# S5 parameter tables in compact form, passed from engine to engine one job slot later

## The chip, the core and the metric

The kernel runs on one core of one Trainium2 chip. A core has TensorE (PE in the profile, its weight loads PEld), VectorE (DVE), ScalarE (ACT), GpSimd (POOL) and SyncE (SP), which here issues every DMA. Each engine works through its own queue in order and waits for the others by semaphores. The metric is the device time of one execution in microseconds (us), as a median over runs.

## What is computed

One step of a two-layer decoder for 512 prompt tokens and 8 x 4 sample tokens, 544 columns in all, model width 1024. Layer 0 mixes tokens by gated linear attention, layer 1 by an S5 state-space layer; each is followed by a squared-ReLU MLP of width 4096. All of it is normed before and after, in fp32:

```
x = x + post_norm(mixer(pre_norm(x)))
x = x + post_norm(square(relu(pre_norm(x) @ w_up)) @ w_down)
```

The change concerns the parameters of the S5 mixer. Of 64 groups with 64 complex states and 16 channels each:

```
dt = exp(log_step);  mag = exp(ar * dt)
lam = mag * (cos(ai * dt) + i sin(ai * dt))
z = (lam - 1) / (ar + i ai);  bb = z * b
h[t] = lam * h[t-1] + bb @ u[t];  y[t] = Re(c @ h[t]) + d * u[t]
```

The kernel does four time steps at once. For that it needs, per pair of groups, W (z times powers of lam times b, to bring four steps of u into the state), Q (powers of lam times c, to read the state out), K (c lam^k bb between the four steps, with d on its diagonal) and the cosine and sine of the angle of lam^4 at 128 multiples, by which states are turned so that the recurrence itself is real.

## The kernel before

**Jobs.** Weights come as 184 tiles of 128 x 1024 fp32. Each tile is split into two parts that TensorE takes: `wh`, the rounded value (a cast by ScalarE, line 111), and `wl = raw - wh` (VectorE line 113, POOL line 115). The activations are split likewise, into a high and a low part (`xh` and `xl`, in the MLP `hh` and `hl`). A job is one tile times one half of the columns (288 or 256): eight blocks of three products, 24 matmuls on line 186. `PLAN` lists the 368 jobs, in blocks of four tiles (8 jobs) or eight (16 jobs). They are numbered from 0 here; the MLP of layer 0 holds jobs 64 to 191, up and down phases of 16 jobs in turn.

**The split of weights.** `plan()` places each tile's split ahead of its first job, in two halves of 512 columns: a tile has its ring slot (`RING` = 5) only when the tile five places earlier has had its last job. In a steady run of blocks of four, the eight jobs of a block get 1, 1, 1, 0, 0, 1, 2 and 2 halves, and a tile's first job follows its first half by 4 to 7 jobs. `job()` calls `split_w` at a job's start: cast, low part, and with the second half the load of the tile three further on (line 93). `dve_ks` says how many of a half's four 128-column slices VectorE subtracts; POOL does the others.

**A job's end.** `finish()` issues the evacuation of the job's sums, then what was deferred to this job, then one entry of `bg`, the background list. In an up phase the evacuation is r = max(sums, 0) * scale by VectorE (line 350), a square and the cast to `hh` by ScalarE (352, 353), and `hl` = r - hh by VectorE (354, deferred to the end of the same job). In a down phase it is one addition into `acc` by VectorE (362).

**The tables.** `s5_prepare` fills `bg` from job 80: one entry a job. Entries 0 to 10 compute dt, mag, lam, z and masks, mostly on POOL, and end in `z_rows`; seven rests; `z_turn` transposes z on TensorE and sets `dve_ks` to `DD[1]` (before it, it is `DD[0]`). From entry 21 on (job 101) come 16 units of four slots, to job 164; a unit is two pairs of groups:

- slot A: W's products (POOL 1008 and 1009, VectorE 1010 and 1011), the angle's first lines (VectorE 1069 to 1071);
- slot B: W's sums (1016, 1017) and its DMA to the scratch tensor `wd`; the angle's reduction (1077, 1078, 1080, 872); loads for the next unit;
- slot C: Q's products on POOL (1029, 1030); sine on ScalarE (1085), the cosine's argument on VectorE (876 to 878);
- slot D: the K products of the unit before on TensorE (1052), its copy by ScalarE (1055) and diagonal by VectorE (1058); Q on VectorE (1035 to 1038), masked bb by ScalarE (1044), cosine (1089), and their DMAs to `qd`, `md` and `wd`.

The two groups of a pair keep to their own halves of a table by zeros. Before, these zeros go through the arithmetic: masks `gm` are multiplied into z and the powers of lam, and W and Q are computed at full width, zeros with them.

The S5 stage, after the MLP, loads W, Q, K and the angles back, u by u.

Of the kernel before, what the change touches and what calls it, by code (L numbers as in the profile page):

```python
# [55 lines left out]
DD = (4,0)  # L56
# [16 lines left out]
class Builder:  # L73
    def __init__(self, tc, io):
        self.tc, self.nc, self.io = tc, tc.nc, io
        self.jobs = 0
        self.after = defaultdict(list)
        self.before_evac = defaultdict(list)
        self.hold, self.held = set(), []
        self.n_tiles = io["w"].shape[0]  # L80
        self.raw, self.wh, self.wl = {}, {}, {}
        self.tile0 = 0
        self.plan()
        self.dve_ks = 1
        self.bg = []
        self.dve_win = None
        self.part = {}
# [8 lines left out]
    def split_w(self, t, part=None):  # L96
# [7 lines left out]
        if part == 0:  # L104
# [6 lines left out]
        nc.scalar.activation(h[:, a:c], r[:, a:c], AF.Copy)  # L111
# [96 lines left out]
    def finish(self, ps, evac):  # L208
        j = self.jobs
        if j in self.hold:  # L210
# [130 lines left out]
    def mlp(self, g_post, g_next, sink=None, after_first=None, before_last=None):  # L341
# [4 lines left out]
        def up(m, hf, ps):  # L346
# [7 lines left out]
            self.defer(0, lambda: nc.vector.tensor_sub(hl[:, m, c0:c1], r[:, :n], f32(h)))  # L354
# [451 lines left out]
    def s5_prepare(self, ctx):  # L806
# [4 lines left out]
        sm = p.tile([128, 26, 32], F32, name="sm")  # L811
# [4 lines left out]
        ldb = p.tile([128, 2, 32, 16], F32, tag="q", name="ldb")  # L816
        ldc = p.tile([128, 2, 32, 16], F32, name="ldc")
        tmp = p.tile([128, 640], F32, name="tmp")
        gm = p.tile([128, 2], F32, name="gm")
        dsk = p.tile([32, 32], F32, name="dsk")  # L820
        iota = p.tile([128, 128], F32, name="iota")
        lp = p.tile([128, 2, 32, 5], F32, tag="cs", name="lp")
        l5 = p.tile([128, 2, 32, 10], F32, name="l5")
        eye = self.cst[0:32, C_ID:C_ID + 32]

        self.kk = [p.tile([32, 2, 256], F32, name=f"kk{i}") for i in (0,)]

# [115 lines left out]

        def masks():
            for r in (0, 1):
                o = l5[:, r].rearrange("p q (t g) -> p q t g", g=2)
                for g in (0, 1):
                    G.tensor_scalar(o[:, :, :, g], lp[:, r], gm[:, g:g + 1], None, op0=OP.mult)
# [4 lines left out]
        def z_rows():  # L953

            z4 = p.tile([128, 2, 32, 4], F32, tag="w", name="z4")
            zm = p.tile([128, 2, 16, 8, 2], F32, tag="q", name="zm")
# [4 lines left out]
            for r in (0, 1):  # L961
                src = z4[:, r].rearrange("p (u q) s -> p u s q", q=2)
                dst = zm[:, r].rearrange("p u (s g) q -> p u s g q", g=2)
                for g in (0, 1):
                    for q in (0, 1):
                        G.tensor_scalar(dst[:, :, :, g, q], src[:, :, :, q], gm[:, g:g + 1], None, op0=OP.mult)
            st["zm"] = zm

        def z_turn():
# [3 lines left out]
            zt = p.tile([128, 512], F32, tag="zb", name="zt")  # L973
            for i in range(4):
                r, hf = divmod(i, 2)
                nc.tensor.transpose(ps[:, i * 128:(i + 1) * 128],
                                    zm[:, r, 8 * hf:8 * hf + 8].rearrange("p u s q -> p (u s q)"),
                                    self.cst[:, C_ID:C_ID + 128])
            nc.scalar.activation(zt, ps, AF.Copy)
            for i in range(4):  # L980
                r, hf = divmod(i, 2)
                nc.sync.dma_start(zd[8 * hf:8 * hf + 8, :, r].rearrange("u s q n -> (u s) q n"),
                                  zt[:, i * 128:(i + 1) * 128])

        def bbar():
            o = p.tile([128, 2, 32, 16], F32, name="bb")
            self.bb = o
# [4 lines left out]
            G.tensor_scalar(ldc[:, 1], ldc[:, 1], -1.0, None, op0=OP.mult)  # L992

        def unit_w(u):
            zb = p.tile([128, 2, 2, 128], F32, tag="zb", name="zb")
            bt = p.tile([128, 2, 2, 64], F32, tag="bt", name="bt")
            src = zd[u].rearrange("s r q n -> s (r q n)")[:, None, :].to_broadcast([8, 16, 512])
            nc.sync.dma_start(zb.rearrange("p r q n -> p (r q n)"), src)
            nc.sync.dma_start(bt, io["s5bt"][:, u])
            st["zb"], st["bt"] = zb, bt  # L1000

        def unit_w2(u):
            w = p.tile([128, 2, 2, 2, 64], F32, tag="w", name="w")
            zb = st["zb"].rearrange("p r q (g n) -> p r q g n", g=2)
            b = [st["bt"][:, r, :, None, :].to_broadcast([128, 2, 2, 64]) for r in (0, 1)]
            zr, zi = zb[:, 0], zb[:, 1]
            tp = [tmp[:, 256 * i:256 * (i + 1)].rearrange("p (q g n) -> p q g n", q=2, g=2) for i in (0, 1)]
            G.tensor_mul(tp[0], zi, b[1])
            G.tensor_mul(tp[1], zi, b[0])
            V.tensor_mul(w[:, 0], zr, b[0])  # L1010
            V.tensor_mul(w[:, 1], zr, b[1])
            st["w"], st["tp"] = w, tp

        def unit_w3(u):
            w, tp = st["w"], st["tp"]
            V.tensor_sub(w[:, 0], w[:, 0], tp[0])
# [3 lines left out]
        def q_parts(u):  # L1020
            sh = [128, 2, 10, 16]
            l = [l5[:, r, 2 * u:2 * u + 2, :, None].to_broadcast(sh) for r in (0, 1)]
            c = [ldc[:, r, 2 * u:2 * u + 2, None, :].to_broadcast(sh) for r in (0, 1)]
            tp = [tmp[:, 320 * i:320 * (i + 1)].rearrange("p (q t c) -> p q t c", q=2, t=10) for i in (0, 1)]
            return l, c, tp

        def unit_q0(u):
            l, c, tp = q_parts(u)
            G.tensor_mul(tp[0], l[1], c[1])
            G.tensor_mul(tp[1], l[1], c[0])  # L1030

        def unit_q(u):
            q5 = p.tile([128, 2, 2, 10, 16], F32, tag="q", name="q5")
            l, c, tp = q_parts(u)
# [4 lines left out]
            nc.sync.dma_start(self.qd[u].rearrange("p (a b) -> p a b", a=4),  # L1039
                              q5.rearrange("p r q t c -> p (r q) (t c)")[:, :, 0:128])  # L1040
            bbd = p.tile([128, 2, 2, 2, 16], F32, tag="bbd", name="bbd")
            for r in (0, 1):
                for g in (0, 1):
                    nc.scalar.activation(bbd[:, r, :, g], self.bb[:, r, 2 * u:2 * u + 2], AF.Copy, scale=gm[:, g:g + 1])
            st["q5"], st["bbd"] = q5, bbd

        def unit_k(u):
            ps = self.bank("kp")
            q5, bbd = st["q5"], st["bbd"]
            for q in (0, 1):  # L1050
                for r in (0, 1):
                    nc.tensor.matmul(ps[0:32, q * 128:(q + 1) * 128], bbd[:, r, q].rearrange("p g c -> p (g c)"),
                                     q5[:, r, q, 2:10].rearrange("p t c -> p (t c)"), start=(r == 0), stop=(r == 1))
            kk = self.kk[0]
            nc.scalar.activation(kk[:, :, 0:128], ps[0:32, 0:256].rearrange("p (q n) -> p q n", q=2), AF.Copy)
            for q in (0, 1):
                o = kk[:, q, 96:128]
                V.scalar_tensor_tensor(o, eye, dsk[:, 2 * u + q:2 * u + q + 1], o, op0=OP.mult, op1=OP.add)
                nc.sync.dma_start(self.md[2 * u + q], kk[:, q])

        E1 = np.float32(np.round(2 * np.pi * 16384) / 16384)
        E2 = float(2 * np.pi - float(E1))

        def unit_t(u):
# [3 lines left out]
            for q in (0, 1):  # L1068
                V.tensor_scalar(m[:, q], iota, col("ptu", q), MAGIC, op0=OP.mult, op1=OP.add)
                V.tensor_scalar(a[:, q], iota, col("phi", q), None, op0=OP.mult)  # L1070
            V.tensor_scalar(m, m, MAGIC, None, op0=OP.subtract)
            st["a"], st["m"] = a, m

        def unit_t2(u):
            a, m = st["a"], st["m"]
            col = lambda n, q: t(n)[:, 2 * u + q:2 * u + q + 1]
            V.scalar_tensor_tensor(a, m, -float(E1), a, op0=OP.mult, op1=OP.add)
            V.scalar_tensor_tensor(a, m, -E2, a, op0=OP.mult, op1=OP.add)
            for q in (0, 1):
                V.scalar_tensor_tensor(a[:, q], iota, col("plo", q), a[:, q], op0=OP.mult, op1=OP.add)  # L1080
            sin_arg(V, a)

        def unit_s(u):
            st["cs"] = p.tile([128, 2, 2, 128], F32, tag="cs", name="cs")
            nc.scalar.activation(st["cs"][:, 1], st["a"], AF.Sin)
            cos_arg(V, st["a"], st["m"])

        def unit_c(u):
# [433 lines left out]
```

## Time and profile before

| what | value |
|---|---|
| median of 3 runs | 1404.31 us (1402.98 to 1405.43) |
| the profiled execution | 1405.15 us; its span, first to last instruction, 1403.4 us |
| granted TensorE clock, mean | 0.968 |
| DMA | 157.53 MB in 79274 packets, 112 GB/s |

The page's groups read: line, engine, operation, written tile <- read tiles, shapes, count | busy us of the group, mean ns of one | idle us of the engine just before, and what ended it. A row of the waits reads: who waited <- for whom: us in total, times, longest. A row of the timeline reads: start us, us, engine, line, operation, and in brackets how long the engine sat idle before it and what ended that. A busy TensorE is not one at its peak: matmuls overlap, so a matmul of 290 ns starts 119 to 133 ns after the one before. It slows down when the granted clock falls.

### The profile page before, as it was taken

The numbers are of one execution on the slowest core, as the hardware profiler recorded it, in microseconds if no ns is written. First come the engines' busy times: TensorE is split into PE (matmuls) and PEld (weight loads), VectorE is DVE, ScalarE is ACT, GpSimd is POOL, SyncE is SP. The second block draws the span as 40 slices with busy tenths as digits, with TensorE's granted clock in tenths as the row PEclk, the third lists the DMA queues.
The fourth block names the chain that finished last, engine by engine and source line by source line (L and its number), as shares of the span: only waits on it lengthen the run. The fifth ranks groups of instructions, "written<-read, shape, count | busy, mean of one in ns | idle before, by whom it ended". The sixth has DMA issues, their size and how long they took to land. (4 is left out here: it accounts for less than half of the span.)

```text
span 1403.4 us, 25744 instructions
## 1 busy us (share of the span) xinstructions
PE 1312.2 (94%) x9968; PEld 1278.3 (91%) x9968; DVE 874.9 (62%) x1793; ACT 563.5 (40%) x1283; POOL 639.5 (46%) x715
## 2 busy tenths in 40 slices
PE   7999999989999898889898997899899999999996
PEld 6999999979999797789897997899799999999996
DVE  7865655597437997799648789655871342332345
ACT  6534354645333423323443332344452432432432
POOL 4443344565474674466445343443643333333240
PEclk9999999999999899999999999999999999999998
DMA  5233222312333454445332768432223232323221
GB/s 184 95 120 124 76 95 64 121 61 77 109 109 113 134 162 132 130 141 175 117 106 72 239 183 254 132 99 91 85 66 91 73 109 69 98 76 106 76 61 64
DMA packets 79274, 157.53 MB, mean 112 GB/s; under 512 B 8144, under 2 KB 41808, under 8 KB 78128
## 3 DMA queue, kind: packets, MB, share of 16 engines
q1 hardware_dynamic: 79152, 155.89, 35.6%
q8 instruction: 78, 1.28, 0.4%
q14 instruction: 44, 0.36, 0.1%
HBM read 130.27 MB, written 25.59 MB: 111 GB/s over the span
## 5 line engine op out<-in xcount | busy, mean ns | idle before, releaser
L115 POOL TENSOR_TENSOR wl<-raw,wh 128x384 fp32r<-128x384 f32 (+2 forms) x351 | 422.4, 1217 | 483.9 <-ACT wh L111 482.1
L111 ACT ACTIVATE wh<-raw 128x512 fp32r<-128x512 f32 x368 | 216.3, 618 | 86.5 <-PE held L186 53.4
L186 PE MATMUL held<-xh,wh 128*128 128x288 f32 (+1 forms) x784 | 233.0, 297 | 2.9 <-ACT wh L111 2.8
L186 PE MATMUL held<-xh,wl 128*128 128x288 f32 (+1 forms) x784 | 229.7, 293 | 3.8 <-POOL wl L115 3.8
L186 PE MATMUL held<-xl,wh 128*128 128x288 f32 (+1 forms) x784 | 230.1, 294 | 0.8 <-DVE xl L279 0.8
L186 PE MATMUL mm<-xh,wh 128*128 128x256 f32 (+1 forms) x752 | 221.8, 295 | 0.8 <-ACT wh L111 0.8
L186 PE MATMUL mm<-xl,wh 128*128 128x256 f32 (+1 forms) x752 | 220.1, 293 | 2.1 <-DVE xl L279 2.0
L186 PE MATMUL mm<-xh,wl 128*128 128x256 f32 (+1 forms) x752 | 218.5, 290 | 0.9 <-POOL wl L115 0.9
L113 DVE TENSOR_TENSOR wl<-raw,wh 128x128 fp32r<-128x128 f32 (+2 forms) x247 | 138.2, 568 | 105.6 <-ACT wh L111 100.2
L186 PEld LDWEIGHTS held<-xh,wl 128*128 128x128 f32 x784 | 150.3, 192 | 5.1 <-POOL wl L115 5.1
L186 PEld LDWEIGHTS held<-xh,wh 128*128 128x128 f32 x784 | 150.8, 192 | 4.6 <-ACT wh L111 3.0
L186 PE MATMUL held<-hh,wh 128*128 128x288 f32 (+1 forms) x512 | 150.4, 294 | 4.0 <-ACT wh L111 4.0
L186 PE MATMUL held<-hh,wl 128*128 128x288 f32 (+1 forms) x512 | 150.2, 293 | 3.1 <-POOL wl L115 3.1
L186 PEld LDWEIGHTS held<-xl,wh 128*128 128x128 f32 x784 | 150.7, 192 | 1.4 <-DVE xl L279 1.0
L352 ACT ACTIVATE r<-r 128x256 f32<-128x256 f32 (+1 forms) x128 | 55.1, 431 | 238.3 <-DVE r L350 238.3
L186 PE MATMUL mm<-hh,wh 128*128 128x256 f32 (+1 forms) x512 | 148.8, 291 | 1.7 <-ACT wh L111 1.7
L186 PE MATMUL held<-hl,wh 128*128 128x288 f32 (+1 forms) x512 | 150.0, 293 | 0.0
L186 PE MATMUL mm<-hh,wl 128*128 128x256 f32 (+1 forms) x512 | 148.2, 290 | 1.8 <-POOL wl L115 1.8
L186 PE MATMUL mm<-hl,wh 128*128 128x256 f32 (+1 forms) x512 | 148.8, 291 | 0.0
L186 PEld LDWEIGHTS mm<-xl,wh 128*128 128x128 f32 x752 | 144.8, 193 | 3.4 <-DVE xl L279 3.2
L186 PEld LDWEIGHTS mm<-xh,wh 128*128 128x128 f32 x752 | 145.1, 193 | 2.7 <-issue 1.2
L186 PEld LDWEIGHTS mm<-xh,wl 128*128 128x128 f32 x752 | 144.1, 192 | 1.1 <-POOL wl L115 1.1
(400 smaller groups left out, 2876.1 us busy)
## 6 DMA issues: line engine op xcount, KB each, us to landing
raw<-in_w SPq DMA_DIRECT2D x184, 512.0 KB
S<-in_h SPq DMA_DIRECT2D x4, 1024.0 KB
out_gla_s<-S SPq DMA_DIRECT2D x4, 1024.0 KB
zb<-zd SPq DMA_DIRECT2D x16, 256.0 KB
wd<-w SPq DMA_DIRECT2D x16, 256.0 KB
qd<-q SPq DMA_DIRECT2D x16, 256.0 KB
wd<-cs SPq DMA_DIRECT2D x16, 256.0 KB
qt<-qd SPq DMA_DIRECT2D x16, 256.0 KB
```

Source lines behind the costliest of these rows:

```text
L111: nc.scalar.activation(h[:, a:c], r[:, a:c], AF.Copy)
L113: nc.vector.tensor_sub(l[:, a:b], r[:, a:b], f32(h[:, a:b]))
L115: nc.gpsimd.tensor_sub(l[:, b:c], r[:, b:c], f32(h[:, b:c]))
L186: self.nc.tensor.matmul(ps[:, :c1 - c0], a[:, k], b[:, k, c0:c1], start=(k == 0 and i == 0), stop=(k == KD - 1 and i == 2))
L352: nc.scalar.activation(r[:, :n], r[:, :n], AF.Square)
```

## The change

1. **Compact tables.** W and Q are computed without the zeros (256 and 320 columns a part become 128 and 160). Two ScalarE copies each (`set_blocks`) put the two groups' halves into one buffer, `blk`, that was zeroed once and is written out from there. The masks and the ten-column powers `l5` are gone; `bb` is held twice over, and K is masked once when it leaves PSUM.
2. **Engines and slots.** W's and Q's products all go to VectorE; the angle's first two lines go to ScalarE (with scale and `MAGIC` as bias), its reduction is done in turns (three VectorE steps and a clip), and the cosine is the sine of pi/2 minus the absolute value, all on ScalarE. What one engine makes in one slot, the next uses in a later one. K's zero half in `md` is filled once by a DMA, in slot 10.
3. **Low parts.** `DD` goes from (4,0) to (4,3): in the units VectorE takes three of four slices of every low part, POOL one, where POOL had all four.
4. **Casts.** While `bg` is not empty, `finish` issues the weight casts of the next job before the evacuation. The subtractions stay at the job's start.
5. **hl.** It goes to a list, `late`, that is run after the `bg` entry.
6. The partition order of W's rows changes, and with it the access patterns of `md` and `ud` in the S5 stage.

```diff
-DD = (4,0)
+DD = (4,3)
...
-        nc.scalar.activation(h[:, a:c], r[:, a:c], AF.Copy)
+        if (t, part) not in self.is_cast:
+            nc.scalar.activation(h[:, a:c], r[:, a:c], AF.Copy)
+        if cast_only:
+            self.is_cast.add((t, part))
+            return
...
     def finish(self, ps, evac):
         j = self.jobs
+        if self.bg:
+            for u in self.split_at.get(self.wjob, []):
+                self.split_w(*u, cast_only=True)
...
         if self.bg:
             for f in self.bg.pop(0):
                 f()
+        for f in self.late:
+            f()
+        self.late.clear()
...
-            self.defer(0, lambda: nc.vector.tensor_sub(hl[:, m, c0:c1], r[:, :n], f32(h)))
+            self.late.append(lambda: nc.vector.tensor_sub(hl[:, m, c0:c1], r[:, :n], f32(h)))
...
+        def zeros():
+            G.memset(blk, 0.0)
+            z = blk[0:32, 0:128]
+            nc.sync.dma_start(self.md.rearrange("u r c -> r u c")[:, :, 128:256], z[:, None].to_broadcast([32, 32, 128]))
...
             for r in (0, 1):
-                src = z4[:, r].rearrange("p (u q) s -> p u s q", q=2)
-                dst = zm[:, r].rearrange("p u (s g) q -> p u s g q", g=2)
-                for g in (0, 1):
-                    for q in (0, 1):
-                        G.tensor_scalar(dst[:, :, :, g, q], src[:, :, :, q], gm[:, g:g + 1], None, op0=OP.mult)
+                G.tensor_copy(zm[:, r], z4[:, r].rearrange("p (u q) s -> p u s q", q=2))
...
+        def set_blocks(full, compact):
+            for g in (0, 1):
+                h = slice(64 * g, 64 * g + 64)
+                nc.scalar.activation(full[h, ..., g, :], compact[h], AF.Copy)
...
-            G.tensor_mul(tp[0], zi, b[1])
-            G.tensor_mul(tp[1], zi, b[0])
-            V.tensor_mul(w[:, 0], zr, b[0])
-            V.tensor_mul(w[:, 1], zr, b[1])
+            V.tensor_mul(w, zb[:, 0][:, None].to_broadcast([128, 2, 2, 64]), b)
+            V.tensor_mul(tp, zb[:, 1][:, None].to_broadcast([128, 2, 2, 64]), b)
+            V.tensor_sub(w[:, 0], w[:, 0], tp[:, 1])
+            V.tensor_add(w[:, 1], w[:, 1], tp[:, 0])
...
         def unit_w3(u):
-            V.tensor_sub(w[:, 0], w[:, 0], tp[0])
-            V.tensor_add(w[:, 1], w[:, 1], tp[1])
-            nc.sync.dma_start(self.wd[u][:, 0:512], w.rearrange("p r q g n -> p (r q g n)"))
+            set_blocks(wf, st["w"].rearrange("p r q n -> p (r q) n"))
+            nc.sync.dma_start(self.wd[u][:, 0:512], wf.rearrange("p a g n -> p (a g n)"))
...
+        def unit_k2(u):
+            V.tensor_mul(kk.rearrange("p q (t n) -> p (q t) n", n=32), st["kp"][0:32, 0:256].rearrange("p (a n) -> p a n", n=32),
+                         same.rearrange("p g c -> p (g c)")[:, None].to_broadcast([32, 8, 32]))
...
         def unit_t(u):
             for q in (0, 1):
-                V.tensor_scalar(m[:, q], iota, col("ptu", q), MAGIC, op0=OP.mult, op1=OP.add)
-                V.tensor_scalar(a[:, q], iota, col("phi", q), None, op0=OP.mult)
-            V.tensor_scalar(m, m, MAGIC, None, op0=OP.subtract)
+                nc.scalar.activation(m[:, q], iota, AF.Copy, scale=col("tu", q), bias=MAGIC)
+                nc.scalar.activation(a[:, q], iota, AF.Copy, scale=col("x", q))
...
         def unit_t2(u):
-            V.scalar_tensor_tensor(a, m, -float(E1), a, op0=OP.mult, op1=OP.add)
-            V.scalar_tensor_tensor(a, m, -E2, a, op0=OP.mult, op1=OP.add)
+            V.scalar_tensor_tensor(a, m, MAGIC, a, op0=OP.subtract, op1=OP.subtract)
             for q in (0, 1):
-                V.scalar_tensor_tensor(a[:, q], iota, col("plo", q), a[:, q], op0=OP.mult, op1=OP.add)
-            sin_arg(V, a)
+                V.scalar_tensor_tensor(a[:, q], iota, t("nr")[:, 2 * u + q:2 * u + q + 1], a[:, q], op0=OP.mult, op1=OP.add)
+            V.tensor_scalar(a, a, 0.5, -0.5, op0=OP.min, op1=OP.max)
 
         def unit_s(u):
-            nc.scalar.activation(st["cs"][:, 1], st["a"], AF.Sin)
-            cos_arg(V, st["a"], st["m"])
+            nc.scalar.activation(cs[:, 1], st["a"], AF.Sin, scale=-TURN)
+            nc.scalar.activation(st["m"], st["a"], AF.Abs)
+            nc.scalar.activation(cs[:, 0], st["m"], AF.Sin, scale=-TURN, bias=t("half_pi")[:, 0:1])
...
-        todo = [load, rest, step_size, magnitude, angles, lams, zs, turn_angle, masks, bbar, z_rows,
+        todo = [load, rest, step_size, magnitude, angles, lams, zs, turn_angle, rest, bbar, [z_rows, zeros],
...
-                     [lambda u=u: unit_q0(u), lambda u=u: unit_s(u)],
-                     ([lambda u=u: unit_k(u - 1)] if u else []) + [lambda u=u: unit_q(u), lambda u=u: unit_c(u)]]
-        todo += [rest, rest, lambda: unit_k(15)]
+                     [lambda u=u: unit_q(u), lambda u=u: unit_s(u)] + ([lambda u=u: unit_k(u - 1)] if u else []),
+                     ([lambda u=u: unit_k2(u - 1)] if u else []) + [lambda u=u: unit_q2(u)]]
+        todo += [rest, rest, lambda: unit_k(15), lambda: unit_k2(15)]
```

More of the change, by code (lines that the diff above doesn't have):

```diff
@@ L81, in __init__ @@
         self.raw, self.wh, self.wl = {}, {}, {}
+        self.is_cast, self.late = set(), []
         self.tile0 = 0
@@ L94, in load_raw, with split_w @@
             self.raw[t] = r
-    def split_w(self, t, part=None):
+    def split_w(self, t, part=None, cast_only=False):
         if part is None:
@@ L103, in split_w @@
         r = self.raw[t]
-        if part == 0:
+        if part == 0 and (t, 0) not in self.is_cast:
             pool = self.p_x if self.in_x[t] else self.p_w
@@ L810, in s5_prepare @@
         V, G = nc.vector, nc.gpsimd
-        sm = p.tile([128, 26, 32], F32, name="sm")
+        sm = p.tile([128, 27, 32], F32, name="sm")
         names = {}
@@ L955, in z_rows @@
             z4 = p.tile([128, 2, 32, 4], F32, tag="w", name="z4")
-            zm = p.tile([128, 2, 16, 8, 2], F32, tag="q", name="zm")
+            zm = p.tile([128, 2, 16, 4, 2], F32, tag="q", name="zm")
             sh = [128, 32, 4]
@@ L1000, in unit_w @@
+            nc.sync.dma_start(bt, io["s5bt"][:, u].rearrange("(s e) r q n -> e s (r q n)", s=4))
             st["zb"], st["bt"] = zb, bt
         def unit_w2(u):
[L1003 to L1007, printed above, removed]
@@ L1027, in unit_q0 @@
[L1027 to L1034, printed above, removed]
+            w = p.tile([128, 2, 2, 64], F32, tag="w", name="w")
+            zb, b = st["zb"], st["bt"]
+            tp = tmp[:, :256].rearrange("p (r q n) -> p r q n", r=2, q=2)
+            V.tensor_mul(w, zb[:, 0][:, None].to_broadcast([128, 2, 2, 64]), b)
@@ L1038, in unit_q, with unit_q2 @@
             V.tensor_sub(q5[:, 1], q5[:, 1], tp[1])
[L1039 to L1045, printed above, removed]
+            st["q5"] = q5
+        def unit_q2(u):
+            set_blocks(qf, st["q5"].rearrange("p r q t c -> p (r q) t c"))
+            nc.sync.dma_start(self.qd[u].rearrange("p (a b) -> p a b", a=4), qf.rearrange("p a t g c -> p a (t g c)")[:, :, 0:128])
         def unit_k(u):
-            ps = self.bank("kp")
-            q5, bbd = st["q5"], st["bbd"]
+            ps = st["kp"] = self.bank("kp")
             for q in (0, 1):
                 for r in (0, 1):
[L1052 to L1055, printed above, removed]
+                    nc.tensor.matmul(ps[0:32, q * 128:(q + 1) * 128], self.bb[:, r, 2 * u + q].rearrange("p g c -> p (g c)"),
+                                     qf[:, 2 * r + q, 1:5].rearrange("p t g c -> p (t g c)"), start=(r == 0), stop=(r == 1))
+        def unit_k2(u):
+            V.tensor_mul(kk.rearrange("p q (t n) -> p (q t) n", n=32), st["kp"][0:32, 0:256].rearrange("p (a n) -> p a n", n=32),
+                         same.rearrange("p g c -> p (g c)")[:, None].to_broadcast([32, 8, 32]))
             for q in (0, 1):
@@ L1377, in run @@
             dp = pool("scratch", space=DRAM)
-            self.zd = dp.tile([16, 8, 2, 2, 128], F32, name="zd")
+            self.zd = dp.tile([2, 16, 4, 2, 2, 64], F32, name="zd")
             self.wd = dp.tile([16, 128, 1024], F32, name="wd")
```

103 lines of the change are left out of this document (51 added, 52 removed).

## The prediction

> **What bounds the kernel now.** I read the page first. TensorE is busy nearly all the time, so a change to the S5 tables can only win time where TensorE waits for the engines that make them.
>
> ```profile
> span 1403.4 us, 25744 instructions
> PE 1312.2 (94%) x9968; PEld 1278.3 (91%) x9968; DVE 874.9 (62%) x1793; ACT 563.5 (40%) x1283; POOL 639.5 (46%) x715
> ```
>
> The windows view comes next. I cut it at the first matmul of the layer-0 MLP's first down blocks (353.15), 16 jobs later (401.57) and 80 jobs after that (709.61). The tables are made in these 96 jobs. The columns are length, then busy time and instructions of each engine, the granted clock, and DMA.
>
> ```profile
> core 0: us, PE busy (x) PEld busy (x) DVE busy (x) ACT busy (x) POOL busy (x), PEclk, DMA share, GB/s
> 353.15:401.57 48.42, 48.42 (x387) 48.42 (x386) 20.62 (x58) 17.14 (x38) 30.32 (x75) 1.00 0.32 101
> 401.57:709.61 308.04, 278.62 (x2055) 266.72 (x2054) 246.27 (x498) 111.55 (x288) 174.36 (x156) 0.95 0.43 134
> ```
>
> The first 16 jobs run without a gap, at full clock: 48.42 us, or 3.03 us a job. The next 80 have the same mix, half of 288 and half of 256 columns, so they would need 5 x 48.42 = 242.1 us. In them lie also the small products for K (line 1052):
>
> ```profile
> L1052 PE MATMUL held<-q,bbd 128*32 128x128 f32 x72 | 10.4, 291 | 5.1 <-DVE q L1037 5.1
> L1052 PE MATMUL kp<-q,bbd 128*32 128x128 f32 x56 | 8.5, 295 | 5.4 <-DVE q L1037 5.4
> ```
>
> That is 18.9 us, 1.2 us for each of 16 units. The floor is 242.1 + 18.9 = 261.0 us, against 308.0: 47 us are lost. TensorE is idle for 308.04 - 278.62 = 29.4 us of them; the rest is matmuls at the lower clock that follows each stop (0.95 on average). 47 us is all that this change can win here.
>
> Who causes the loss? First the list of waits over the 80 jobs, then one stop in order of time.
>
> ```profile
> ACT r L352 <- DVE r L350: 112.9, 45, 5.2
> POOL wl L115 <- ACT wh L111: 105.3, 35, 8.7
> DVE hl L354 <- ACT hh L353: 45.3, 47, 1.0
> PE held L186 <- POOL wl L115: 6.9, 8, 1.1
> PE held L186 <- ACT wh L111: 6.8, 3, 2.8
> ```
> ```profile
> 561.26 1.51 DVE L1077 SCALAR_TENSOR_TENSOR ta<-tm,ta 128x256 f32<-128x256 f32 x1
> 562.80 0.84 DVE L1078 SCALAR_TENSOR_TENSOR ta<-tm,ta 128x256 f32<-128x256 f32 x1
> 563.68 0.96 DVE L1080 SCALAR_TENSOR_TENSOR ta<-iota,sm,ta 128x128 f32<-128x128 f32 x2
> 564.89 0.42 DVE L350 SCALAR_TENSOR_TENSOR r<-mm,rs 128x256 f32<-128x256 f32 x1
> 565.34 0.42 ACT L352 ACTIVATE r<-r 128x256 f32<-128x256 f32 x1 [5.16 <-DVE r L350]
> 566.41 0.61 ACT L111 ACTIVATE wh<-raw 128x512 fp32r<-128x512 f32 x1
> 567.08 0.45 PE L186 MATMUL held<-xh,wh 128*128 128x288 f32 x1 [2.79 <-ACT wh L111]
> ```
>
> Read this backwards. TensorE stops at 564.3 for a weight cast (line 111). The cast stands in ScalarE's queue behind the square of an evacuation, which waited 5.16 us for VectorE's r. That r stands in VectorE's queue behind the S5 angles. So VectorE is the bound, and ScalarE, idle itself, carries its delay into the weights. How full VectorE is shows in two units of an up phase, from one K evacuation (549.49) to the next but one:
>
> ```profile
> 549.49:587.34 37.85, 29.66 (x202) 27.63 (x203) 29.69 (x64) 14.50 (x39) 18.10 (x16) 0.91 0.38 122
> ```
>
> A unit takes 37.85 / 2 = 18.9 us. VectorE is busy for 29.69 / 2 = 14.8 of it and waits for hh, as the waits say, 45.3 / 47 = 0.96 us in each of four jobs: 14.8 + 3.9 = 18.7, which leaves nothing. TensorE's work in a unit is four jobs and one K: 4 x 3.03 + 1.2 = 13.3. So an up phase loses 5.6 us a unit. Units fill jobs 101 to 164 in the kernel's numbering, and half of these jobs are up jobs: 8 x 5.6 = 45, nearly the 47 above. In a down job the evacuation is one addition with no wait, and there the engine just keeps up.
>
> **The change part by part.** VectorE first. For a unit of an up phase I count what it does afterwards, with these rows:
>
> ```profile
> L1011 DVE TENSOR_TENSOR w<-zb,bt 128x256 f32<-128x256 f32 x16 | 19.6, 1225 | 0.0
> L1016 DVE TENSOR_TENSOR w<-w,tmp 128x256 f32<-128x256 f32 x16 | 6.6, 414 | 0.0
> L1035 DVE TENSOR_TENSOR q<-l,ldc 128x320 f32<-128x320 f32 x16 | 7.6, 474 | 0.0
> L1080 DVE SCALAR_TENSOR_TENSOR ta<-iota,sm,ta 128x128 f32<-128x128 f32 x32 | 15.4, 521 | 0.6
> L872 DVE TENSOR_SCALAR ta<-ta 128x256 f32<-128x256 f32 x16 | 4.7, 294 | 0.5
> L1058 DVE SCALAR_TENSOR_TENSOR kk<-cst,dsk,kk 32x32 f32<-32x32 f32 x32 | 9.8, 341 | 0.0
> L113 DVE TENSOR_TENSOR wl<-raw,wh 128x512 fp32r<-128x512 f32 x17 | 13.4, 814 | 14.1 <-ACT wh L111 13.9
> L350 DVE SCALAR_TENSOR_TENSOR r<-held,rs 128x288 f32<-128x288 f32 x36 | 16.3, 452 | 19.2 <-PE held L186 19.2
> L354 DVE TENSOR_TENSOR hl<-r,hh 128x288 fp32r<-128x288 f32 x64 | 33.5, 524 | 51.3 <-ACT hh L353 51.3
> ```
>
> From 414 ns at 256 columns and 474 at 320 come estimates for other widths: 0.29 us at 128, 0.32 at 160, 0.53 at 384. Then:
> - w: two products of 256 and two sums of 128, 2 x 0.41 + 2 x 0.29 = 1.4 (W's products with zi come over from POOL; all are half as wide as before).
> - angles: one of 256, two of 128 at 0.52, one clip, 0.41 + 1.04 + 0.29 = 1.75. The four iota lines, three steps of the reduction and the cosine's three steps are gone.
> - q: six of 160, 1.9 (two of them were POOL's).
> - K: the masking product and two diagonals, 0.41 + 0.68 = 1.1.
> - low parts of weights, new here: four of 384 columns, since DD = (4,3) gives VectorE three of every four slices. I take 0.55 each, 2.2; three quarters of the 814 ns row bounds it at 0.61, nothing below 0.53.
> - evacuation: 4 x (0.45 + 0.52) = 3.9.
>
> The sum is 12.2 us. Rows overlap at their ends: for the unit before, the same rows add to 16.6 and the busy time was 14.8, a factor of 0.89. So 10.9 us of VectorE stand against TensorE's 13.3. The wait for hh goes too: hl now stands behind at least one us of slot work, while ScalarE squares and copies. What is late next is then nothing on VectorE, unless POOL gets in its way.
>
> That is the open cost. L1011 is the same instruction as L1016, and takes 1225 ns where POOL runs beside it. Afterwards POOL has only a quarter of each low part:
>
> ```profile
> L654 POOL COPY qkx<-glo 128x128 f32<-128x128 f32 x8 | 3.3, 409 | 0.1
> ```
>
> Four such pieces a unit, each holding VectorE for at most its own 0.41 us, add 1.6: 12.5 us, still under 13.3. The Trainium skill ("SBUF — State Buffer", section "SBUF: two separate sides") says that a VectorE instruction with two SBUF inputs and a POOL instruction exclude each other for the whole instruction; the two rows of w agree. It speaks against this change, which gives VectorE more two-input weight work: by it the whole 1.6 us would stay, and the unit take 12.5 us where the rows alone leave it between 10.9 and 12.5.
>
> ScalarE takes the work over.
>
> ```profile
> L111 ACT ACTIVATE wh<-raw 128x512 fp32r<-128x512 f32 x368 | 216.3, 618 | 86.5 <-PE held L186 53.4 <-POOL wl L115 17.0 <-DMA raw<-in_w 15.1
> L403 ACT ACTIVATE acc<-acc,vec 128x256 f32<-128x256 f32 x7 | 3.6, 510 | 0.2
> L1085 ACT ACTIVATE cs<-ta 128x256 f32<-128x256 f32 x16 | 6.6, 410 | 80.5 <-DVE ta L872 80.5
> L240 ACT ACT_TABLE_LOAD x9 | 11.5, 1283 | 0.2
> ```
>
> Per up unit: four casts 2.5; eight evacuation steps at about 0.42, 3.4; two w blocks of 256 and two q blocks of 320, 2 x 0.41 + 2 x 0.46 = 1.7; four angle lines of 128 with a pointer operand, at most 0.51 each, say 0.4, 1.6; sine, absolute value, sine, 1.2. That is 10.4 us against 13.3; before, the two units shown above had 14.50 / 2 = 7.3. It fits. A slot's ScalarE inputs come from the slot before, so nothing there waits inside its own slot.
>
> The casts go ahead of the evacuation: each waits for its tile's load and for its ring slot, which a job's end frees, and the squares (then hh, hl) queue behind it for 0.6 us or twice that. In return a cast no longer waits for VectorE. POOL loses four products and 3/4 of its low parts.
>
> SP issues seven table DMAs a unit before and after (K's two become one, zb's one becomes two); the wait for w is now for ScalarE's blocks, 0.8 us later in the same slot. In slot 10 SP gets something new: the zero fill of md waits for POOL's memset behind z_rows, and the weight loads queue behind it.
>
> ```profile
> 406.56 4.55 POOL L966 TENSOR_SCALAR zm<-z,gm 128x64 f32<-128x64 f32 x8
> 398.07 0.33 SPq L93 DMA_DIRECT2D raw<-in_w  x1
> PE yp L1233 <- DMA m<-md: 8.5, 9, 3.1
> ```
>
> POOL ended z_rows at 411.1; it loses these eight masks and the masks slot and gets two copies and the memset, so I expect the fill at about 406. The load that left at 398.07 then leaves some 8 us later, behind 0.5 MB. It is asked for at the start of job 94, and by the plan its tile's first job is 104, 30 us on, so TensorE does not see it. The S5 stage reads md and ud in another order with as many packets; TensorE waits 8.5 us there for md in all. I take no change, and 4 us either way as its bound.
>
> The sum: 47 us less an allowance of 3 for bursts (a slot with two low parts carries 4 us of VectorE work against a 3.2 us job, given back by the next). 44 us off the profiled execution's own 1405.15 us (its span and 1.8 us around it) is 1361; off the median, 1404.31, it is 1360.3.
>
> **The rivals.** First, VectorE stays too full. If its two-input instructions meet POOL as L1011 did, 0.8 us longer each, w's two products add 1.6 and two of the nine in angles and q another 1.6; the low parts at 0.81 add 1.1: 12.2 + 4.3 = 16.5, times 0.89 is 14.7, 1.4 over 13.3. Eight units keep 11 us: 1404.3 - 47 + 11 = 1368. For it speaks L1011; against it, that POOL has about a quarter of its work left.
>
> Second, ScalarE becomes the bound: the absolute value between two sines could need a table change each way, 2 x 1.283 = 2.6 us a unit. 10.4 + 2.6 = 13.0 is just at 13.3; with delays in order it might cost 2 us in each of 8 units, 1373. The Trainium skill ("ScalarE: Activation LUTs", section "Table sets: the hidden batching unit") lists abs among functions in every set; by that there is no load and the sum stands. No row here shows it beside a sine.
>
> Third, slower: the cast at the head of ScalarE's queue meets a load that has not landed, and holds squares, hl and the next low parts behind it. 40 tiles pass in the 80 jobs; from 1.2 us of TensorE time per tile the win is gone, and at 2 us each it is 1404.3 - 47 + 80 = 1437. Against it: the waits over the 80 jobs name no load for ScalarE.
>
> Fourth, the stop is not VectorE's and about nothing changes, 1404; the stop shown above speaks against it.
>
> **How the numbers follow.** The forecast gets 0.76, the first rival 0.12, the second 0.05, the third 0.03, the fourth 0.04. 0.2% is 2.8 us, about what a measurement of this kernel can tell. Faster: the first three cases and half the fourth, 0.95; the same 0.02, slower 0.03. The range runs from all 47 us plus 2 in S5, 1355, to 1377, which covers the first two rivals with some of the md bound.
>
> **What would show it.** In the changed profile the same 80 jobs should take about 264 us at a clock near 1.00; VectorE under 11 us busy a unit; the waits of TensorE for wh and wl, and of ScalarE for r, nearly gone; no table load between the tables' first sine and the MLP's end. It is wrong if VectorE rows of line 113 stand near 1 us, if ScalarE waits for raw, or if TensorE's idle time in these jobs stays above 10 us.

## The result and the profile after

The changed kernel takes 1358.99 us (median of 4 runs, 1355.28 to 1359.86). The kernel before, timed beside it, takes 1403.64 us (4 runs, 1402.09 to 1405.43). The ratio is 0.9676, with a 95% interval of 0.9655 to 0.9698. The profiled execution took 1359.06 us, at a mean granted clock of 0.978.

The first lines of the page of the changed kernel:

```profile
span 1357.3 us, 25681 instructions
PE 1298.1 (96%) x9966; PEld 1270.3 (94%) x9966; DVE 798.9 (59%) x1779; ACT 602.4 (44%) x1349; POOL 509.9 (38%) x644
```

VectorE and POOL are busy for less, ScalarE for a little more. Where the time went shows in the windows view. I cut the 80 jobs of the prediction, "the stretch" from here on, at every change between up and down phases: jobs 96 to 111 (up), 112 to 127 (down), 128 to 143 (up), 144 to 159 (down), 160 to 175 (up). The kernel before, with the prediction's columns:

```profile
401.57:451.88 50.31, 50.29 (x399) 49.72 (x397) 32.28 (x62) 17.64 (x41) 27.26 (x32) 1.00 0.38 117
451.88:518.05 66.17, 59.00 (x418) 55.84 (x417) 60.34 (x125) 23.59 (x65) 39.63 (x33) 0.92 0.47 146
518.05:585.07 67.02, 57.74 (x419) 54.41 (x418) 54.47 (x112) 22.40 (x59) 35.20 (x32) 0.95 0.44 137
585.07:649.35 64.28, 57.30 (x418) 54.34 (x417) 59.54 (x123) 22.62 (x63) 39.95 (x33) 0.95 0.46 145
649.35:709.61 60.26, 54.28 (x411) 52.42 (x410) 39.63 (x80) 25.31 (x62) 32.31 (x28) 0.94 0.38 121
```

The changed kernel, the same phases:

```profile
401.71:452.61 50.90, 50.90 (x404) 50.20 (x402) 31.41 (x86) 31.13 (x77) 10.03 (x17) 1.00 0.51 152
452.61:505.77 53.16, 53.16 (x417) 51.77 (x416) 36.23 (x106) 28.97 (x67) 9.04 (x17) 1.00 0.55 169
505.77:558.93 53.16, 53.16 (x417) 51.77 (x416) 38.95 (x115) 35.73 (x88) 7.98 (x16) 1.00 0.51 159
558.93:612.09 53.16, 53.16 (x417) 51.76 (x416) 35.00 (x103) 28.17 (x66) 8.47 (x16) 1.00 0.52 164
612.09:662.99 50.90, 50.90 (x402) 50.20 (x401) 28.33 (x74) 25.38 (x58) 8.59 (x14) 1.00 0.36 114
```

TensorE is now busy in every microsecond of the stretch, at full clock. Its five lengths add to 261.28 us, where the prediction's floor was 261.0. The stretch got 308.04 - 261.28 = 46.8 us shorter. Two other stages gave a little back: jobs 80 to 95 take 49.39 us instead of 48.42 (told below), the S5 stage 147.99 instead of 146.98. All other stages together are 1.3 us shorter, and the spans differ by 1403.4 - 1357.3 = 46.1.

The second reading is by phase. Line against line, 13.0, 13.9, 11.1 and 9.4 us went from the last four phases: the two down phases had lost as much as the two up phases.

What the engines wait for in the stretch of the changed kernel:

```profile
POOL wl L120 <- ACT wh L113: 210.9, 63, 15.7
ACT r L363 <- DVE r L361: 46.3, 32, 4.3
DVE hl L365 <- ACT hh L364: 22.7, 20, 7.8
...
DVE acc L373 <- PE held L191: 20.5, 12, 2.2
...
ACT wh L113 <- DMA raw<-in_w: 10.3, 4, 9.6
```

No row has PE on its left, and TensorE's weight loads (PEld) wait 1.0 us for other engines in all. VectorE now waits for TensorE (acc): it has become the engine that has time. ScalarE waits for r 46.3 us in place of 112.9. That is not "nearly gone", as the prediction had it, but TensorE loses nothing by it now.

### The profile page after: what moved, and what is told of

It reads as the page before. It is cut to its first block, busy times and chain, and to the rows that moved or that the text cites. A ratio compares the mean times of both kernels' runs of the same rounds, so it can differ in the third digit from the quotient of the medians.

```text
span 1357.3 us, 25681 instructions
## 1 busy us (share of the span) xinstructions
PE 1298.1 (96%) x9966; PEld 1270.3 (94%) x9966; DVE 798.9 (59%) x1779; ACT 602.4 (44%) x1349; POOL 509.9 (38%) x644
## 5 line engine op out<-in xcount | busy, mean ns | idle before, releaser
L120 POOL TENSOR_TENSOR wl<-raw,wh 128x384 fp32r<-128x384 f32 (+3 forms) x351 | 351.9, 1014 | 597.8 <-ACT wh L113 588.9
L118 DVE TENSOR_TENSOR wl<-raw,wh 128x128 fp32r<-128x128 f32 (+3 forms) x324 | 180.4, 568 | 102.6 <-ACT wh L113 96.6
L191 PE MATMUL held<-xh,wh 128*128 128x256 f32 (+1 forms) x792 | 235.1, 297 | 0.1
L191 PE MATMUL held<-xl,wh 128*128 128x256 f32 (+1 forms) x792 | 232.2, 293 | 0.8 <-DVE xl L290 0.8
L191 PE MATMUL held<-xh,wl 128*128 128x256 f32 (+1 forms) x792 | 230.9, 292 | 0.0
L191 PE MATMUL mm<-xl,wh 128*128 128x288 f32 (+1 forms) x744 | 216.7, 291 | 1.8 <-DVE xl L290 1.8
L191 PE MATMUL mm<-xh,wh 128*128 128x288 f32 (+1 forms) x744 | 218.2, 293 | 0.0
L191 PE MATMUL mm<-xh,wl 128*128 128x288 f32 (+1 forms) x744 | 215.1, 289 | 0.0
L191 PE MATMUL held<-hl,wh 128*128 128x256 f32 (+1 forms) x512 | 148.1, 289 | 0.0
L191 PE MATMUL held<-hh,wh 128*128 128x256 f32 (+1 forms) x512 | 148.0, 289 | 0.0
```

The lines of the kernel that those rows point to most:

```text
L118: nc.vector.tensor_sub(l[:, a:b], r[:, a:b], f32(h[:, a:b]))
L120: nc.gpsimd.tensor_sub(l[:, b:c], r[:, b:c], f32(h[:, b:c]))
L191: self.nc.tensor.matmul(ps[:, :c1 - c0], a[:, k], b[:, k, c0:c1], start=(k == 0 and i == 0), stop=(k == KD - 1 and i == 2))
```

## The experiments

Four theories about where the 47 us came from; the letters are those of the expectations. They do not exclude each other: D says why VectorE's time, which A counts, was as long as it was.

- **A, capacity.** In each unit VectorE's busy time and the waits that it can't avoid must fit into TensorE's 13.3 us. Before they didn't; now they do.
- **B, order.** Casts stood behind evacuations and hl in front of the table work; the reordering (parts 4 and 5 of the change) is what helps.
- **C, tables.** The gain lies in W, Q and K and in handing on one slot later, not in the angles.
- **D, POOL.** VectorE's rows are long because POOL's work holds them up, so what matters is that POOL's products and low parts went away.

All runs at a glance. "Stretch" is jobs 96 to 175 of the profiled execution, with VectorE's and POOL's busy time in it. The kernel before was timed anew beside each group of runs, and each ratio is to its median there: 1403.64 for the changed kernel, 1400.57 for x1 to x3 and y1, 1400.09 for z1, z2, d2 and d5, 1404.11 for p2, y3, y4 and b1.

| kernel | median us | ratio to before (95%) | stretch us | DVE | POOL |
|---|---|---|---|---|---|
| before | 1403.64 | 1 | 308.0 | 246.3 | 174.4 |
| x1: before, casts first | 1403.18 | 1.0008 (0.9989 to 1.0027) | 309.9 | 245.6 | 165.9 |
| x2: before, hl last | 1391.80 | 0.9931 (0.9904 to 0.9959) | 298.5 | 249.8 | 174.8 |
| x3: before, both | 1391.76 | 0.9927 (0.9898 to 0.9956) | 299.1 | 249.8 | 168.5 |
| z1: before, new angles | 1366.91 | 0.9755 (0.9672 to 0.9838) | 272.8 | 195.3 | 173.9 |
| after | 1358.99 | 0.9676 (0.9655 to 0.9698) | 261.3 | 169.9 | 44.1 |
| y1: after, hl early | 1358.37 | 0.9696 (0.9668 to 0.9724) | 261.7 | 170.0 | 47.0 |
| y3: after, old order | 1359.65 | 0.9708 (0.9677 to 0.9739) | 263.2 | 172.6 | 58.7 |
| z2: after, old angles | 1359.72 | 0.9704 (0.9645 to 0.9763) | 262.8 | 208.2 | 50.5 |
| y4: after, low parts on POOL | 1359.26 | 0.9693 (0.9662 to 0.9724) | 261.3 | 177.1 | 103.9 |
| d2: after, VectorE load 2 | 1360.19 | 0.9707 (0.9649 to 0.9765) | 263.6 | 228.8 | 48.2 |
| d5: after, VectorE load 5 | 1453.83 | 1.0375 (1.0312 to 1.0438) | 361.0 | 322.4 | 50.9 |
| p2: d2 and POOL load | 1422.39 | 1.0143 (1.0108 to 1.0179) | 323.4 | 290.4 | 172.2 |
| b1: after, rest of turn_angle later | 1355.90 | 0.9671 (0.9648 to 0.9695) | 261.3 | 171.3 | 44.3 |

### The order of the work, alone

x1 is the kernel before with part 4 alone:

```diff
+        if self.bg:
+            for u in self.split_at.get(self.wjob, []):
+                self.split_w(*u, cast_only=True)
         if j in self.hold:
```

> The kernel before, with one part of the change alone: the weight casts of the next job go ahead of the evacuation. VectorE's work is unchanged. Theory A (VectorE's capacity: 18.7 us of work and forced waits in an up unit against TensorE's 13.3): TensorE only changes what it waits for (hh, hl, K in place of weights), 30 to 45 of the 47 us lost stay, 1388 to 1402 us. Theory B (queue order: weights stand behind squares that wait for VectorE): the loss goes with the order, at most 10 us stay, 1357 to 1367 us.

It brought nothing: 1403.18 us, 1 us beyond A's range and far from B's. Waits from the list over x1's stretch:

```profile
DVE hl L362 <- ACT hh L361: 45.1, 47, 1.0
...
PE kp L1060 <- DVE q L1045: 11.2, 3, 3.8
PE held L1060 <- DVE q L1045: 10.8, 6, 7.1
```

The casts no longer wait for r, so TensorE waits less for late weights (10.4 us, 18.9 before). But VectorE is as late as before, and TensorE stops at K's products instead, which wait for VectorE's q (22.0 us, 10.5 before). The chain that the prediction read backwards was only the way by which the lateness arrived.

x2 is part 5 alone:

```diff
+        for f in self.late:
+            f()
+        self.late.clear()
...
-            self.defer(0, lambda: nc.vector.tensor_sub(hl[:, m, c0:c1], r[:, :n], f32(h)))
+            self.late.append(lambda: nc.vector.tensor_sub(hl[:, m, c0:c1], r[:, :n], f32(h)))
```

> The kernel before, with hl alone moved behind the background entry; tables and casts as before. Theory A: VectorE no longer waits 0.96 us for hh in each up job, so an up unit needs 14.8 us of it, 1.5 over 13.3; over 8 such units 12 us stay lost at most: 1357 to 1371 us. Theory B: the casts still stand behind squares that wait for r, so most of the loss stays, 1385 us or more.

VectorE's waits over x2's stretch:

```profile
DVE hl L358 <- ACT hh L357: 13.6, 14, 1.0
DVE kk L1062 <- ACT kk L1059: 9.8, 8, 1.3
DVE ta L881 <- ACT cs L1089: 8.5, 8, 1.1
```

The wait for hh fell from 45.3 to 13.6 us, but two steps that need ScalarE's work of the same slot now reach the head of VectorE's queue too early: K's diagonal, which reads what ScalarE copies, and the cosine's argument, which overwrites what the sine reads. They never waited before. Busy time and forced waits add to 246.3 + 45.3 = 291.6 us before and to 249.8 + 13.6 + 9.8 + 8.5 = 281.7 here, 9.9 less. The stretch got 9.6 shorter. So A's sum holds, but its range (1357 to 1371) missed: x2 took 1391.80, since I had not seen the waits behind hl. B's range for x2, 1385 or more, was met; x1 is the run that speaks against B. x3, both parts on the kernel before:

> The kernel before, with both reorderings and none of the compact tables. Theory A: as with hl last alone or a little under, since the weights no longer carry a lag: 1357 to 1369 us. Theory B: 1357 to 1365 us. If both hold, the tables themselves gave little of the 45 us.

It is x2 again (299.1 against 298.5 us), and at 1391.76 both ranges missed, for the same reason. From the other end, y1 is the changed kernel with hl back in its old place (x2's last two lines the other way round), and y3 is y1 with the three lines of x1 taken out as well.

> The changed kernel with hl put back ahead of the background entry. Theory A: VectorE's 9.7 us of busy time in an up unit and four waits of 0.96 us make 13.6, 0.3 over TensorE's 13.3: 0 to 4 us slower than the changed kernel, 1359 to 1363. Theory B: the casts go first, so nothing changes, 1359.

> The changed kernel with both reorderings undone: casts at the job's start behind the evacuation, hl ahead of the background entry. Theories A and D: VectorE needs at most 12.7 us in an up unit (9.8 and four waits of 0.7 to 0.96), r comes on time and so do the casts: 0 to 4 us slower than the changed kernel, 1358 to 1363. If the order matters by itself, 10 us or more.

The stretch of y1 is 0.4 us longer than that of the changed kernel, y3's 1.9 us; neither is visible in the medians. B is out: both reorderings together are worth 9 us where VectorE is full and at most 2 where it isn't.

### The angles, alone and left out

z1 is the kernel before with the changed kernel's angles (`turn_angle`, `unit_t`, `unit_t2`, `unit_s`; `unit_c` gone), z2 the changed kernel with the old ones. The core of z1, and of z2 the other way round:

```diff
-                V.tensor_scalar(m[:, q], iota, col("ptu", q), MAGIC, op0=OP.mult, op1=OP.add)
-                V.tensor_scalar(a[:, q], iota, col("phi", q), None, op0=OP.mult)
-            V.tensor_scalar(m, m, MAGIC, None, op0=OP.subtract)
+                nc.scalar.activation(m[:, q], iota, AF.Copy, scale=col("tu", q), bias=MAGIC)
+                nc.scalar.activation(a[:, q], iota, AF.Copy, scale=col("x", q))
...
-            V.scalar_tensor_tensor(a, m, -float(E1), a, op0=OP.mult, op1=OP.add)
-            V.scalar_tensor_tensor(a, m, -E2, a, op0=OP.mult, op1=OP.add)
+            V.scalar_tensor_tensor(a, m, MAGIC, a, op0=OP.subtract, op1=OP.subtract)
```

> The kernel before with the new angle steps alone (first lines on ScalarE, reduction in turns, cosine by the absolute value); W, Q, K, casts and hl as before. Theory A (VectorE's capacity, its work and its forced waits): the ten old VectorE angle instructions of a unit add to 7.3 us by their rows, the four new ones to 1.5; times 0.89 that frees 5.2, so an up unit needs 18.7 - 5.2 = 13.5 against 13.3 and 2 to 8 us stay lost of 47: 1358 to 1366 us. Rival C (the gain lies in W, Q, K and in handing on one slot later): a third of the gain at most, 1387 us or more.

> The changed kernel with the old angle steps put back, all else changed. Theory A: an up unit takes 9.8 + 5.2 = 15.0 us of VectorE, a down unit about 14.1, against 13.3: 8 x 1.7 + 8 x 0.8 = 20 us slower than the changed kernel, 1370 to 1385 us. Rival C: at most a third of the gain goes, 1359 to 1374 us.

z1 wins 308.0 - 272.8 = 35.2 of the 46.8 us; at 1366.91 it is 1 us beyond A's range, and 20 below C's. But z2, which gives these steps back, loses only 1.5. The two overlap: the angles alone bring three quarters, and everything else without them nearly all. A's number for z2 missed; C's range for z2 was met, but z1 leaves no room for C. A took the old angle steps at what they had cost before, and in z2 they add only 208.2 - 169.9 = 38.3 us, 2.4 a unit. The same two lines before, by shortest, median and longest:

```profile
L1069 DVE TENSOR_SCALAR tm<-iota,sm x32: 272/513/1323, 425.0 to 670.4; 128x128 f32<-128x128 f32 x32
```

and in z2:

```profile
L1075 DVE TENSOR_SCALAR tm<-iota,sm x32: 269/278/474, 427.6 to 621.5; 128x128 f32<-128x128 f32 x32
```

Instruction and shape are the same, the median is half. What differs around them is above all POOL: 174.4 us busy before, 50.5 in z2. The trace of the kernel before points there too. Of these 32 instructions, the 16 that ran with no POOL instruction beside them took 272 to 277 ns, the 16 with one 749 to 1323. This is what made me form D.

### How much VectorE can take

d2 and d5 add idle work to the changed kernel: n products of 320 columns at the end of each slot, 2 or 5, read by nobody.

```diff
+        def load_v():
+            for _ in range(2):
+                V.tensor_mul(tmp, lc[:, 0:320], lc[:, 320:640])
...
-            todo += [[lambda u=u: unit_w2(u), lambda u=u: unit_t(u)],
+            todo += [[lambda u=u: unit_w2(u), lambda u=u: unit_t(u), load_v],
```

> The changed kernel with two idle products of 320 columns added on VectorE in each slot (eight a unit, 0.40 us from start to start: 3.2 us), the result unused. Theory A: an up unit goes from 9.8 to 13.0 us against 13.3, so this is hidden: 0 to 4 us slower, 1359 to 1363 us. If VectorE's delay passes on before it is full, 10 us or more are lost.

> The same with five products a slot, 8.0 us a unit. Theory A: 17.8 us in an up unit and 16.8 in a down unit against 13.3, 8 x 4.5 + 8 x 3.5 = 64 us, less up to 10 that lags into the rests at the end: 1413 to 1423 us. If VectorE's capacity is not the bound, far less.

Jobs 112 to 159 of d2, three phases with four units each:

```profile
452.29:505.71 53.42, 53.32 (x417) 51.70 (x416) 51.97 (x139) 30.12 (x72) 10.97 (x19) 1.00 0.55 164
505.71:558.87 53.16, 53.16 (x417) 51.77 (x416) 51.85 (x143) 34.09 (x82) 7.74 (x14) 1.00 0.52 160
558.87:612.09 53.22, 53.22 (x418) 51.79 (x417) 51.75 (x139) 29.92 (x73) 10.79 (x18) 1.00 0.51 163
```

VectorE is busy for 51.85 of 53.16 us, 13.0 a unit, and TensorE loses 0.3 us in the three phases. The whole stretch is 2.3 us longer than that of the changed kernel, 2.0 of it in jobs 96 to 111: there VectorE waits 4.1 us for the first unit's load of `bt`, and TensorE stops later for 1.5. The changed kernel has the same wait (4.5 us) and loses nothing by it. Jobs 128 to 143 of d5:

```profile
535.24:619.27 84.03, 62.05 (x418) 57.51 (x417) 80.80 (x204) 36.11 (x87) 10.60 (x18) 0.89 0.35 105
```

Now TensorE follows VectorE. The size of d5 missed (1453.83 us), since I had taken a product at 0.40 us from start to start. Its row took 0.51 on average, and VectorE's busy time grew by (322.4 - 169.9) / 320 = 0.48 for each:

```profile
L1101 DVE TENSOR_TENSOR tmp<-ldc 128x320 f32<-128x320 f32 x320 | 164.2, 513 | 9.8
```

Twenty a unit are 10.2 us. With 9.7 us of own work in an up unit (38.95 / 4) and 8.9 in a down unit (36.23 + 35.00 over 8), eight units of each lose 8 x (9.7 + 10.2 - 13.3) + 8 x (8.9 + 10.2 - 13.3) = 99 us. Measured: 361.0 - 261.3 = 99.7. That the two agree so closely is partly luck: the up jobs lost 61.7 us, where this counts 52.8, and the down jobs 38.1, where it counts 46.4. In sum it is A: next to nothing lost up to TensorE's time, about full price beyond it.

### POOL's part

p2 is d2 with two products a slot on POOL, read by nobody, sized to bring POOL's busy time back to that of the kernel before:

```diff
+            for _ in range(2):
+                q = self.p_t.tile([128, 288], F32, tag="sq", name="pd", bufs=5)
+                G.tensor_mul(q, lc[:, 0:288], lc[:, 288:576])
```

> The changed kernel with the two idle VectorE products a slot, which alone cost nothing, and two idle POOL products of 288 columns beside them (results unused; nothing waits for them). Theory A, own work only: VectorE has no instruction more than with its two products alone and TensorE waits for nothing of POOL's, so 1358 to 1362 us. Theory D (much of VectorE's time before was waiting for POOL's instructions, inside its own rows: about 80 us over the units, with POOL busy for 174): POOL gets 64 x 2 x 0.85 = 109 us more, about 4 us a unit that VectorE's rows grow by, 17 us against 13.3: 40 to 65 us slower, 1400 to 1425 us.

62 us slower than d2 by the medians, 59.8 in the stretch. VectorE runs the same 608 instructions in it, in 290.4 us instead of 228.8. Three of its rows in d2:

```profile
L1101 DVE TENSOR_TENSOR tmp<-ldc 128x320 f32<-128x320 f32 x128 | 63.8, 498 | 3.3
L118 DVE TENSOR_TENSOR wl<-raw,wh 128x384 fp32r<-128x384 f32 x77 | 45.6, 612 | 0.3
...
L1028 DVE TENSOR_TENSOR w<-w,tmp 128x128 f32<-128x128 f32 x16 | 4.8, 301 | 0.6
```

The same rows in p2:

```profile
L1101 DVE TENSOR_TENSOR tmp<-ldc 128x320 f32<-128x320 f32 x128 | 75.7, 591 | 3.3
L118 DVE TENSOR_TENSOR wl<-raw,wh 128x384 fp32r<-128x384 f32 x77 | 57.2, 762 | 0.3
...
L1028 DVE TENSOR_TENSOR w<-w,tmp 128x128 f32<-128x128 f32 x16 | 11.1, 693 | 0.6
```

and the row on POOL that was added, with nobody waiting for its result:

```profile
L1104 POOL TENSOR_TENSOR pd<-ldc 128x288 f32<-128x288 f32 x128 | 123.4, 989 | 0.0
```

D is shown: with VectorE full, 123 us of idle work on POOL cost 60 us of the kernel. TensorE waits in p2 for VectorE's low parts (29.4 us) and for ScalarE's blocks (12.0), never for POOL. D alone is not the whole, for z1 won 35.2 us with POOL as busy as before. The Trainium skill ("SBUF — State Buffer", section "SBUF: two separate sides") says that a VectorE instruction in a mode that uses two ports, or with two SBUF inputs beside a POOL instruction that reads SBUF, and the POOL instruction exclude each other for the whole instruction. The two-input rows here agree. L1069 reads one tensor and was held up as well; whether it ran in such a mode no run here shows. A VectorE row that reads PSUM, line 361, kept its time in p2: in the stretch its means are 413 and 447 ns for 256 and 288 columns, 415 and 450 in d2. Over the whole run (shortest, median, longest):

```profile
L361 DVE SCALAR_TENSOR_TENSOR r<-mm,rs x65: 406/425/459, 304.1 to 1362.4; 128x256 f32<-128x256 f32 x34, 128x288 f32<-128x288 f32 x31
```

y4 gives the low parts back to POOL:

```diff
-DD = (4,3)
+DD = (4,0)
```

> The changed kernel with DD = (4,0): POOL makes all low parts in the units, as before the change. Theory A, own work only: VectorE loses 43 us of work, its busy time falls by that, 1357 to 1361 us. Theory D: POOL is busy about 75 us more and VectorE's other rows grow by 25 us or more, so its busy time falls by less than 20 us; that still fits beside TensorE, 1357 to 1364 us.

VectorE loses the 42.8 us of line 118's 384-column row, yet its busy time rises from 169.9 to 177.1. Three rows of the changed kernel:

```profile
L118 DVE TENSOR_TENSOR wl<-raw,wh 128x384 fp32r<-128x384 f32 x77 | 42.8, 576 | 0.4
...
L1027 DVE TENSOR_TENSOR tmp<-zb,bt 128x256 f32<-128x256 f32 x16 | 8.4, 522 | 0.0
...
L1029 DVE TENSOR_TENSOR w<-w,tmp 128x128 f32<-128x128 f32 x16 | 4.8, 300 | 0.0
```

and in y4:

```profile
L1029 DVE TENSOR_TENSOR w<-w,tmp 128x128 f32<-128x128 f32 x16 | 13.3, 832 | 0.0
L1027 DVE TENSOR_TENSOR tmp<-zb,bt 128x256 f32<-128x256 f32 x16 | 13.2, 825 | 0.0
```

So part 3 of the change is free for VectorE: what it subtracts itself it no longer waits for. TensorE sees neither, since both fit.

### The stop in job 91

The prediction did not foresee the 1 us that jobs 80 to 95 lost. The timeline of the changed kernel there:

```profile
386.67 0.67 DVE L959 SCALAR_TENSOR_TENSOR sm<-sm 128x32 f32<-128x32 f32 x3 [2.17 <-POOL sm L957]
387.37 0.19 DVE L960 TENSOR_TENSOR sm<-sm 128x32 f32<-128x32 f32 x1
387.59 0.18 DVE L961 TENSOR_SCALAR sm<-sm 128x32 f32<-128x32 f32 x1
387.69 2.14 DVE L118 TENSOR_TENSOR wl<-raw,wh 128x512 fp32r<-128x512 f32 x2
...
388.86 0.41 PE L191 MATMUL mm<-hh,wl 128*128 128x288 f32 x1 [0.71 <-DVE wl L118]
```

`turn_angle` now has five VectorE instructions at the end of its angle work. The first of them waits 2.17 us for POOL, at the head of VectorE's queue, and a low part that TensorE needs waits behind it. b1 puts the five lines into an entry of their own, seven slots later (14 instead of 7):

```diff
+        def turn_rest():
+            for i, d in enumerate((D1, D2, D3)):
...
-                *[rest] * 7, z_turn, rest, lambda: unit_w(0)]
+                *[rest] * 3, turn_rest, *[rest] * 3, z_turn, rest, lambda: unit_w(0)]
```

> The changed kernel with the five VectorE lines of turn_angle moved from slot 7 into a rest, slot 14, by when POOL has long made their inputs. TensorE's stop in job 91 (0.71 us idle and a slower clock, 1.0 us in all) goes; 1 us faster than the changed kernel by the spans of the 16 jobs, too little for the median to tell.

The stop is gone: jobs 80 to 95 take 48.41 us. By its median b1 is the fastest kernel here, but its runs (1354.53 to 1358.39) overlap those of the changed kernel and the ratios differ by less than their intervals, so that the 1 us is seen in the trace alone.

## Why the prediction was right

- **The bound.** VectorE, not TensorE, set the pace, and 47 us were lost to it. Shown by d2 and d5 (idle work on VectorE is free or costs its time, by how full VectorE is) and by x1 (the queue through which it arrives does not matter). All 46.8 us went, down to 261.28 us where the floor was 261.0. The 3 us held back for bursts weren't needed there, but 2.0 were lost in jobs 80 to 95 and in the S5 stage. So the medians differ by 44.65 us where 44 were forecast; that it came so close is partly luck.
- **"8 x 5.6 = 45", and "in a down job ... the engine just keeps up".** This cross-check of the 47 (the forecast itself goes by the floor) was right by offsetting errors, which is luck. The two units that I measured were the worst of their phase: jobs 128 to 143 lost 13.9 us, 3.5 a unit. And down units lost 12.1 / 4 = 3.0 each, as VectorE was busy there too for 60.34 + 4.7 (its wait for hh) of 66.17 us. Over all 16 units it is 46.8 / 16 = 2.9 on average; one pair of units was too little to read a rate from.
- **VectorE's new work.** 38.95 / 4 = 9.7 us per up unit, where the sum gave 10.9 and POOL's pieces up to 1.6 more. The low part of 384 columns took 576 ns (0.55 taken), w's sums of 128 columns 0.30 and 0.31 (0.29). The first rival asked for 0.8 us more per two-input row; line 118's largest group stayed within 0.03 us of what was taken, with POOL busy for only 44 of the 261 us. W's second product (L1027, 522 ns) was held up by 0.1.
- **ScalarE.** 35.73 / 4 = 8.9 us per up unit against 10.4. The rows that it took over, in the stretch of the changed kernel:

```profile
L1011 ACT ACTIVATE blk<-q 64x320 f32<-64x320 f32 x32 | 14.8, 462 | 2.3 <-DVE q L1047 2.2
...
L1077 ACT ACTIVATE tm<-iota,sm 128x128 f32<-128x128 f32 x32 | 12.4, 387 | 0.0
...
L1093 ACT ACTIVATE tm<-ta 128x256 f32<-128x256 f32 x16 | 6.4, 402 | 0.0
```

- **The second rival** is refuted: L1093 is the absolute value between two sines, and no table load lies in the stretch. The Trainium skill ("ScalarE: Activation LUTs", section "Table sets: the hidden batching unit") has abs in every set, and the trace agrees.
- **The third rival** happened without its price. A cast did meet a late load once, 9.6 us behind the zero fill, which left at 404.89 (predicted about 406). hl then waited 7.8 us behind it, and TensorE lost nothing, as the tile was due much later. One tile of 40, not all.
- **"The wait for hh goes too."** In the busiest phase (jobs 128 to 143) 0.5 us of it are left, but 22.7 in the stretch: 9.0 after the last units' slots, where VectorE has nothing else to do, and most of the rest behind that one late cast. By y1 it would have cost nothing in its old place either.
- **POOL.** I had priced it as a cost of the new kernel (1.6 us a unit). It was rather a large part of what the change removed. Over VectorE's rows in the stretch, count x (mean - shortest of that form) adds to 64 us before and 11 after; L1010 and L1011, which never ran below 943 ns where their like took 412, hide 2 x 16 x 0.53 = 17 more, and L1078 (835, in z2 424) another 7. So an estimated 85 to 90 us of VectorE's time before were its own rows held up. That POOL's work does this is shown by p2 and y4; for the kernel before, the sum is worked out from its rows. Not every row beside POOL is held up: L1038 had POOL beside it all 16 times before, and kept its 473 ns.
- **What stays open.** How the relief divides between POOL's products and its low parts was not tried on the kernel before. The 1 us more in the S5 stage is inside the 4 us bound, and the same stage spreads from 146.4 to 151.2 us over the profiles of all these kernels.

## What to carry to other kernels

Per period, add up the busy time of the engine that feeds the pacing one and the waits that it can't avoid: in these runs next to nothing was lost below the pacing engine's time and about all of the excess above it, and the order of the queues mattered only there. Before counting instructions, compare the mean of a VectorE row with its shortest: a wide gap, in a stretch where POOL is busy, is a reason to suspect POOL, and a row that never ran alone shows no gap, so compare it with others of its shape. Then moving work off POOL, even onto VectorE, can be free, as part 3 was here. Read such a rate over whole phases, not from the one place that looks worst.

## What had not been expected of the hardware

- VectorE's time for the same work is not a constant: 228.8 or 290.4 us for the same 608 instructions, by POOL's work beside it, which nobody read.
- It isn't only the rows with two tensors: the row with one (L1069) ranged from 272 to 1323 ns before, and all of the slow ones had POOL at work beside them.
- TensorE can stand right beside a nearly full VectorE: in jobs 112 to 159, VectorE was busy for 13.0 us a unit in d2 and a unit took 13.3 us, TensorE's own time. In p2 16.6 us busy made it 17.0, in d5 18.3 made it 19.0. Nothing between 13.0 and 16.6 was run.
